# MLP block products on one NeuronCore: joined 512-column matmuls, sums on GpSimd, and a reordered tail

## The chip, the cores and the metric

The kernel runs on one core of a Trainium2 chip. Its time is the device time of one execution in microseconds (us). All inputs are laid out on the host beforehand and lie in the chip's memory; the output is written there.

## The reference

One layer of an encoder: a mixing block, then an MLP, then a final RMSNorm, for 512 tokens of width 2048, in float32. The change touches the MLP and the final norm only.

```python
h = h + mixed @ w_out
hn = _rmsnorm(h, norm_mlp_w)
h = h + jnp.square(jax.nn.relu(hn @ w_mlp_up)) @ w_mlp_down     # 2048 -> 8192 -> 2048
return _rmsnorm(h, norm_final_w)
```

## The kernel before

Everything is held transposed: features lie on the 128 partitions, the 512 tokens along the free axis. To keep float32 precision with fast matmuls, each operand is split into a rounded part (hi) and the remainder (lo), and a product is hi x hi + hi x lo + lo x hi. `split` does it: ScalarE casts the tile to hi, VectorE subtracts hi from the tile and writes lo (lines 94, 95).

**The MLP is computed by blocks.** Two blocks of weights' rows by two of columns (A11, A12, A21, A22) meet two halves of 256 tokens. Seven products of sums of blocks take the place of eight products of blocks: Q4, P1, P5, P6, P3, P7, P2. The weights' sums S1 to S4 are four VectorE additions of 128x1024 tiles (`run_product`), and each of the seven operands is split. The other side of a product is a tile `XS` of 128x512: columns 0 to 255 (`lo_t`) hold the hi part of one operand, columns 256 to 511 (`hi_t`) its lo part. `product` runs 8 contraction steps j, each with three matmuls of 256 columns: weights hi by X hi (line 904), the same weights hi by X lo (line 905), weights lo by X hi (line 906). All three add up in the same 256 columns of a PSUM bank. A pair has three banks, a, b and c, in which several products accumulate one after the other; after each product the bank's running value is read out.

**Up** (2048 to 8192): 32 pairs u0 to u31, one after the other (the first two and the last two interleaved). `up_evac` reads each product out: ScalarE copies Q4, P5, P1 and P6 into `tA` and `tB`, VectorE adds P7, P3 and P2 to those straight out of PSUM into the results `r0` and `r1`. VectorE then applies relu and the norm's factor `rB`, ScalarE squares. `differences` forms on VectorE the sums of token halves that the down projection needs, and the SyncE queue writes them to memory (`hidD`).

**Down** (8192 to 2048): 4 rounds b of 8 pairs, two pairs at a time. At a round's beginning `operand_fill` loads 56 tiles of 128x256 from `hidD` and splits them into `XS`. Each product is added by VectorE out of PSUM to a tile `h0` or `h1` (loaded from `hTD`) and stored back by `store`, in the last round also squared and summed into `acc`. The last two pairs of the last round (`keep`) run in another order, and `tail` and `finish` follow them with the final norm, half by half: the four tiles' squares, their column sums on TensorE (`stat2`), the reciprocal root on VectorE, then 16 scaled tiles of 128x256, five by GpSimd (line 1148) and eleven by VectorE (line 1150), and 16 DMAs to `out` on the SyncE queue (line 1151).

Tiles come from pools with a fixed number of buffers (3 for each of `wh` and `wl`, the split weights; 7 for `a`, the second row of weight blocks). Each engine takes its instructions in one fixed order, which is set when the program is built, from the data's dependences and from the free buffers; an instruction whose input or buffer is not ready holds up what stands behind it on its engine.

Of the kernel before, what the change touches and what calls it, by code (L numbers as in the profile page):

```python
# [49 lines left out]
def tile_hybrid_block(  # L50
# [733 lines left out]
    with ExitStack() as p1:  # L784
# [76 lines left out]
        with ExitStack() as p5:  # L861
# [36 lines left out]

            def product(ps, w, o, first=False):
                hi, lo = w  # L900
                for j in range(8):
                    t = XS[o, j]
                    c = slice(j * 128, (j + 1) * 128)
                    PE.matmul(ps, hi[:, c], t[:, lo_t], start=first and j == 0, stop=False, skip_group_check=True)  # L904
# [16 lines left out]
            def open_pair(nm, a11, a12):  # L921
                p = Pair()
                p.nm, p.ps, p.step = nm, {}, 0
                p.a11, p.a12 = a11, a12
                p.keep = False
                return p

            def run_product(p, q, sums):
# [27 lines left out]
                if bk not in p.ps:  # L956
                    p.ps[bk] = bank()[:, 0:256]
                product(p.ps[bk], w, ROLE[q], q in FIRST)
                return p.ps[bk]

# [7 lines left out]

            def up_evac(i, p, q, et):
                ps = p.ps[BANK[q]]  # L970
                if not hasattr(p, "tA"):
                    p.tA, p.tB = et(f"tA_u{i}"), et(f"tB_u{i}")
                    p.r0, p.r1 = ev(f"r0_u{i}"), ev(f"r1_u{i}")
                    p.left = 7
                tA, tB, r0, r1 = p.tA, p.tB, p.r0, p.r1
                if q == "Q4":
                    S_.copy(out=tA[:, 0], in_=ps)
                elif q == "P5":
                    S_.copy(out=tA[:, 1], in_=ps)
                elif q == "P1":  # L980
                    S_.copy(out=tB[:, 0], in_=ps)
                elif q == "P6":
                    S_.copy(out=tB[:, 1], in_=ps)  # L983
                elif q == "P7":
                    add(r1.rearrange("p (o t) -> p o t", o=2), ps[:, None, :].to_broadcast([128, 2, 256]), tA)
                    V.scalar_tensor_tensor(out=r1, in0=r1, scalar=0.0, in1=rB, op0=ALU.min, op1=ALU.mult)
                    S_.activation(out=r1, in_=r1, func=AF.Square)
                elif q == "P3":
                    add(r0[:, hi_t], ps, tB[:, 1])
# [31 lines left out]
            for i, p in enumerate(first):  # L1021
                for q in ("P1", "P2"):
                    w = heads[i, q] or wsplit(p.a12, f"{q}_u{i}")
                    p.ps[BANK[q]] = bank()[:, 0:256]
                    product(p.ps[BANK[q]], w, ROLE[q], True)
# [3 lines left out]
        with ExitStack() as p6:  # L1029
            sm = p6.enter_context(tc.tile_pool(name="sm", bufs=1, side="right", reuse_waits="tile"))  # L1030

            def a_tile(name):
                return sm.tile([128, 1024], F32, tag="a", name=name, bufs=7)

            def et(name):
                return sm.tile([128, 2, 256], F32, tag="et", name=name, bufs=6)

            def more(p, s22, s21):
# [4 lines left out]
            def up_group(idx, order, ps=None):  # L1043
                ps = ps or [up_open(i) for i in idx]
                for i, p in zip(idx, ps):
                    m0, m1 = up_m(i)
                    more(p, wup[m1, 1], wup[m1, 0])
                if order[0] == "P1":
                    for q in ("P1", "P2"):
                        for i, p in zip(idx, ps):  # L1050
                            up_evac(i, p, q, et)
                    order = order[2:]
                for n, q in enumerate(order):
                    for i, p in zip(idx, ps):
# [24 lines left out]
            def down_group(b, idx, order, done):  # L1079
                ps = []  # L1080
                for i in idx:
                    p = open_pair(f"d{b}_{i}", load_raw(wdn[2 * i, 2 * b], f"A11_d{b}_{i}"), load_raw(wdn[2 * i, 2 * b + 1], f"A12_d{b}_{i}"))
                    more(p, wdn[2 * i + 1, 2 * b + 1], wdn[2 * i + 1, 2 * b])
                    p.keep = order is not ORDER
                    ps.append(p)
                for e in (1, 0):
# [57 lines left out]
            def finish(half, ts, sqs):  # L1144
                psf = yield from stat2(f"f{half}", sqs, range(2 * half, 2 * half + 2))
                for m in range(16):
                    if m % 3 == 2:
                        G.tensor_tensor(out=Hf[m][:, ts], in0=Hf[m][:, ts], in1=rB[:, ts], op=ALU.mult)
                    else:
                        V.tensor_tensor(out=Hf[m][:, ts], in0=psf[:, ts], in1=Hf[m][:, ts], op=ALU.mult)  # L1150
                    nc.sync.dma_start(out=out[m * 128 : (m + 1) * 128, ts], in_=Hf[m][:, ts])
                    if half == 0 and m % 4 == 3:
                        yield
# [15 lines left out]
            def tail(i, p, q):  # L1169
                if i != 7 or q not in ("P2", "P3"):  # L1170
                    return
                half = 0 if q == "P2" else 1
                ts = slice(half * 256, half * 256 + 256)
                sqs = []
                for k, x in enumerate(pairs):
                    for e, h in ((0, x.h0), (1, x.h1)):
                        m = 2 * (6 + k) + e
                        sq = tp.tile([128, T], F32, tag="sq", name=f"sqt{m}{half}", bufs=1)
                        S_.activation(out=sq[:, ts], in_=h[:, ts], func=AF.Square)
                        if m < 15:  # L1180
                            add(acc[:, ts], acc[:, ts], sq[:, ts])
                        else:
                            sqs.append(sq)
# [4 lines left out]
                tasks.append(finish(half, ts, sqs))  # L1188

# [95 lines left out]
```

## Time and profile before

| | |
|---|---|
| median of 3 runs | 2886.01 us (2880.28 to 2888.11) |
| the profiled execution, whole | 2884.02 us |
| its span in the trace | 2881.9 us |
| TensorE busy | 2811.9 us, 98% |
| VectorE busy | 2065.1 us, 72% |
| ScalarE busy | 1167.0 us, 40% |
| GpSimd busy | 24.8 us, 1% |

The rows further down come from the profiled execution; its time is 2.0 us below the median of the runs. PE is TensorE's matmuls, PEld its weight loads, DVE VectorE, ACT ScalarE, POOL GpSimd, SPq the DMA issues of SyncE. An instruction's duration is longer than the distance to the next one behind it where the two overlap, so for a rate the distance between starts is read. "Idle ... <-" names what ended a wait.

### The profile page before, as it was taken

To read this page: it belongs to the slowest core of one execution; us is meant where nothing else is said; L and a number is where in the kernel's file an instruction comes from. 1 tells how busy PE (TensorE), PEld (TensorE's weight loads), DVE (VectorE), ACT (ScalarE), POOL (GpSimd) and SP (SyncE) were. 2 spreads that over 40 slices of the span, in tenths; PEclk is the share of its full clock that TensorE was granted. 3 is DMA by queue.
4 is the path that set the end of the run, shared out by engine and by line. 5 is a ranking of instruction groups with operands and counts; after the bars stand their busy time and mean duration, and the time that the engine had idled before them with its cause. 6 is when DMAs were issued, how large, how long until landed. Compare 5 with 4: busy or idle time off the path is not lost.

```text
span 2881.9 us, 45456 instructions
## 1 busy us (share of the span) xinstructions
PE 2811.9 (98%) x17944; PEld 2538.3 (88%) x17944; DVE 2065.1 (72%) x3131; ACT 1167.0 (40%) x1869; POOL 24.8 (1%) x66
## 2 busy tenths in 40 slices
PE   8999999999999999999999999999998999999997
PEld 6778788888788888888888999999998999999997
DVE  6888769845564444444447888888888888898987
ACT  6444322223233333322335444444445354444543
POOL 0000010000000000000000000000000000000000
PEclk9999999999999999999999999999999999999998
DMA  7555663555642222533443445454447566565644
GB/s 228 191 187 189 196 198 120 183 173 182 181 140 93 87 93 84 199 133 125 142 145 137 153 151 156 143 162 147 149 146 228 180 222 201 170 226 174 221 133 146
DMA packets 217493, 469.32 MB, mean 163 GB/s; under 512 B 38976, under 2 KB 80000, under 8 KB 217280
## 3 DMA queue, kind: packets, MB, share of 16 engines
q1 hardware_dynamic: 216608, 464.33, 49.9%
q8 instruction: 140, 2.29, 0.3%
q0 software_dynamic: 672, 2.10, 0.3%
q14 instruction: 73, 0.60, 0.1%
HBM read 379.15 MB, written 87.20 MB: 162 GB/s over the span
## 4 chain that ended last, share of the span: by engine, by line
PE 78%; DMA 9%; DVE 9%; ACT 2%; issue 1%; SPq 0%; DVEq 0%; ACTq 0%
PE ps_b L906 12%; PE ps_b L904 12%; PE ps_b L905 12%; PE ps_mm L115 8%; PE ps_mm L117 8%; PE ps_mm L116 8%; PE ps_b L115 4%; PE ps_b L116 4%; PE ps_b L117 4%; DMA hr<-hidD 1%; DVE wl_S_d L95 1%; DVE wl_in L90 1%; DMA bB<-rowD 1%; DMA hTD<-h 1%; DMA Nd<-bB 1%
## 5 line engine op out<-in xcount | busy, mean ns | idle before, releaser
L115 PE MATMUL ps_mm<-xh,wh_in 128*128 128x512 f32 x1416 | 567.1, 400 | 3.1 <-ACT wh_in L89 3.1
L117 PE MATMUL ps_mm<-xh,wl_in 128*128 128x512 f32 x1416 | 559.9, 395 | 0.5 <-DVE wl_in L90 0.5
L116 PE MATMUL ps_mm<-xl,wh_in 128*128 128x512 f32 x1416 | 559.8, 395 | 0.0
L89 ACT CAST wh_in<-raw_in 128x1024 fp32r<-128x1024 f32 x177 | 186.0, 1051 | 412.9 <-PE ps_mm L116 328.5
L117 PEld LDWEIGHTS ps_mm<-xh,wl_in 128*128 128x128 f32 x1416 | 267.7, 189 | 60.4 <-DVE wl_in L90 1.0
L115 PEld LDWEIGHTS ps_mm<-xh,wh_in 128*128 128x128 f32 x1416 | 267.7, 189 | 58.6 <-ACT wh_in L89 3.5
L116 PEld LDWEIGHTS ps_mm<-xl,wh_in 128*128 128x128 f32 x1416 | 267.7, 189 | 55.0 <-issue 0.2
L90 DVE TENSOR_TENSOR wl_in<-raw_in,wh_in 128x1024 fp32r<-128x1024 f32 x177 | 216.2, 1222 | 118.7 <-ACT wh_in L89 110.2
L904 PE MATMUL ps_b<-XT_h,wh_S_d 128*128 128x256 f32 x768 | 220.8, 287 | 10.6 <-ACT wh_S_d L94 10.6
L906 PE MATMUL ps_b<-XT_h,wl_S_d 128*128 128x256 f32 x768 | 220.9, 288 | 3.2 <-DVE wl_S_d L95 3.1
L905 PE MATMUL ps_b<-XT_h,wh_S_d 128*128 128x256 f32 x768 | 219.8, 286 | 0.0
L906 PE MATMUL ps_b<-XT_x,wl_S_u 128*128 128x256 f32 x768 | 217.4, 283 | 0.8 <-DVE wl_S_u L95 0.8
L904 PE MATMUL ps_b<-XT_x,wh_S_u 128*128 128x256 f32 x768 | 217.4, 283 | 0.5 <-ACT tB_u L983 0.5
L905 PE MATMUL ps_b<-XT_x,wh_S_u 128*128 128x256 f32 x768 | 217.3, 283 | 0.0
L94 ACT CAST wh_S_u<-A_u 128x1024 fp32r<-128x1024 f32 x128 | 134.3, 1050 | 147.2 <-DVE A_u L911 81.2
L94 ACT CAST wh_S_d<-A_d 128x1024 fp32r<-128x1024 f32 x124 | 129.6, 1047 | 148.2 <-PE ps_b L905 129.0
L95 DVE TENSOR_TENSOR wl_S_u<-A_u,wh_S_u 128x1024 fp32r<-128x1024 f32 x128 | 156.0, 1222 | 39.4 <-ACT wh_S_u L94 39.4
L95 DVE TENSOR_TENSOR wl_S_d<-A_d,wh_S_d 128x1024 fp32r<-128x1024 f32 x124 | 151.2, 1222 | 23.9 <-ACT wh_S_d L94 22.2
L904 PEld LDWEIGHTS ps_b<-XT_h,wh_S_d 128*128 128x128 f32 x768 | 149.8, 195 | 12.5 <-ACT wh_S_d L94 12.5
L906 PEld LDWEIGHTS ps_b<-XT_h,wl_S_d 128*128 128x128 f32 x768 | 149.9, 195 | 5.0 <-DVE wl_S_d L95 5.0
L905 PEld LDWEIGHTS ps_b<-XT_h,wh_S_d 128*128 128x128 f32 x768 | 149.9, 195 | 0.0
L906 PEld LDWEIGHTS ps_b<-XT_x,wl_S_u 128*128 128x128 f32 x768 | 147.2, 192 | 1.0 <-DVE wl_S_u L95 1.0
(393 smaller groups left out, 7033.9 us busy)
## 6 DMA issues: line engine op xcount, KB each, us to landing
raw_in<-in_win SPq DMA_DIRECT2D x177, 512.0 KB
raw_A_u<-in_wup SPq DMA_DIRECT2D x64, 512.0 KB
A_u<-in_wup SPq DMA_DIRECT2D x64, 512.0 KB
A_d<-in_wdn SPq DMA_DIRECT2D x64, 512.0 KB
raw_A_d<-in_wdn SPq DMA_DIRECT2D x64, 512.0 KB
raw_wo<-in_wout SPq DMA_DIRECT2D x32, 512.0 KB
h<-hTD SPq DMA_DIRECT2D x64, 256.0 KB
hTD<-h SPq DMA_DIRECT2D x60, 256.0 KB
```

The lines of the kernel that those rows point to most:

```text
L89: S_.copy(out=hi, in_=raw)
L90: V.tensor_tensor(out=lo, in0=raw, in1=hi.bitcast(F32), op=ALU.subtract)
L94: S_.copy(out=hi, in_=src)
L95: V.tensor_tensor(out=lo, in0=src, in1=hi.bitcast(F32), op=ALU.subtract)
L115: PE.matmul(ps, hi[:, w], rh, start=first and kk == 0, stop=False)
L116: PE.matmul(ps, hi[:, w], rl, start=False, stop=False)
L117: PE.matmul(ps, lo[:, w], rh, start=False, stop=last and kk == 7)
L904: PE.matmul(ps, hi[:, c], t[:, lo_t], start=first and j == 0, stop=False, skip_group_check=True)
L905: PE.matmul(ps, hi[:, c], t[:, hi_t], start=False, stop=False, skip_group_check=True)
L906: PE.matmul(ps, lo[:, c], t[:, lo_t], start=False, stop=j == 7, skip_group_check=True)
```

## The change

- **Joined matmuls.** In `product` (new argument `whole`), the two matmuls with the weights' hi part become one of 512 columns over the whole `XS` tile; its result fills a whole bank, hi x hi in the first half and hi x lo in the second. The third stays at 256 columns and adds into the first half. In the last contraction step the two change places.
- **Read-out.** Each of these products is now copied whole (128x512) by ScalarE into a new tile `u` (`spill`, two buffers), and GpSimd (`gsum`, a tensor_tensor) adds up the two halves: per up pair 9 adds of 128x256 and one of 128x512, per down pair 13 and one. VectorE's adds out of PSUM go. This holds for all 32 up pairs and the first 30 down pairs; the last two (`keep`) stay as they were.
- **Buffers.** `a` has 6 buffers where it had 7.
- **Tail.** `tail` takes the square of each of the last four tiles' halves when that half is complete; it no longer scales those four by `nfw_s` on ScalarE. In `finish`, VectorE does this scaling in a scalar_tensor_tensor for tiles 12 to 15, GpSimd has four tiles and VectorE twelve, and in the second half every other output DMA is issued by ScalarE's queue.

```diff
+                    if whole:
+                        mms = [(ps, hi, t), (ps[:, lo_t], lo, t[:, lo_t])]
+                        for n, (dst, a, b) in enumerate(mms if j < 7 else mms[::-1]):
+                            PE.matmul(dst, a[:, c], b, start=first and j + n == 0, stop=j == 7 and n == 1, skip_group_check=True)
...
+            def gsum(out, x, y, op=ALU.add):
+                G.tensor_tensor(out=out, in0=x, in1=y, op=op)
...
+                u = spill(ps, f"u{q}_u{i}")
                 if q == "Q4":
-                    S_.copy(out=tA[:, 0], in_=ps)
+                    gsum(tA[:, 0], u[:, 0], u[:, 1])
                 elif q == "P5":
-                    S_.copy(out=tA[:, 1], in_=ps)
+                    gsum(tA[:, 1], u[:, 0], u[:, 1])
                 elif q == "P7":
-                    add(r1.rearrange("p (o t) -> p o t", o=2), ps[:, None, :].to_broadcast([128, 2, 256]), tA)
+                    gsum(u[:, 0], u[:, 0], u[:, 1])
+                    gsum(r1.rearrange("p (o t) -> p o t", o=2), u[:, 0:1, :].to_broadcast([128, 2, 256]), tA)
...
-                    add(r0[:, lo_t], ps, tB[:, 0])
+                    dst = r0[:, lo_t] if q in ("P1", "P2") else r0[:, hi_t]
+                    gsum(dst, dst if q in ("P2", "P3") else u[:, 1], u[:, 0])
+                    if q in ("P2", "P3"):
+                        gsum(dst, dst, u[:, 1])
...
-                return sm.tile([128, 1024], F32, tag="a", name=name, bufs=7)
+                return sm.tile([128, 1024], F32, tag="a", name=name, bufs=6)
...
+            def spill(ps, name):
+                u = sm.tile([128, 2, 256], F32, tag="pr", name=name, bufs=2)
+                S_.copy(out=u.rearrange("p a b -> p (a b)"), in_=ps)
+                return u
...
+                        if p.whole:
+                            u = spill(t, f"u{q}_{p.nm}")
+                            if q == "P7":
+                                gsum(u[:, 0], u[:, 0], u[:, 1])
+                                hv = h1.rearrange("p (o t) -> p o t", o=2)
+                                gsum(hv, hv, u[:, 0:1, :].to_broadcast([128, 2, 256]), ALU.subtract)
+                            else:
+                                dst = (h1 if q in ("Q4", "P5") else h0)[:, lo_t if q in ("Q4", "P1", "P2") else hi_t]
+                                for k in range(2):
+                                    gsum(dst, dst, u[:, k], ALU.subtract if q in ("Q4", "P5") else ALU.add)
...
+                    queue = nc.scalar if half and m % 2 else nc.sync
+                    queue.dma_start(out=out[m * 128 : (m + 1) * 128, ts], in_=Hf[m][:, ts])
...
-                        S_.activation(out=h[:, ts], in_=h[:, ts], func=AF.Copy, scale=nfw_s[:, m : m + 1])
-                        Hf[m] = h
+                sq = tp.tile([128, T], F32, tag="sq", name=f"sqt{m}{half}", bufs=1)
+                S_.activation(out=sq[:, ts], in_=h[:, ts], func=AF.Square)
+                Hf[m] = h
```

On TensorE, inside an up product, two contraction steps stand like this before (`wh` and `wl` are the weights' hi and lo parts, `XT_x` the operand):

```order
L904 MATMUL ps_b<-XT_x_12070,wh_S_u_14219 128x256
L905 MATMUL ps_b<-XT_x_12070,wh_S_u_14219 128x256
L906 MATMUL ps_b<-XT_x_12070,wl_S_u_14220 128x256
L904 MATMUL ps_b<-XT_x_12071,wh_S_u_14219 128x256
L905 MATMUL ps_b<-XT_x_12071,wh_S_u_14219 128x256
L906 MATMUL ps_b<-XT_x_12071,wl_S_u_14220 128x256
```

And now, the last two steps of a product and the first of the next:

```order
L907 MATMUL ps_b<-XT_x_12052,wh_A_u_14722 128x512
L907 MATMUL ps_b<-XT_x_12052,wl_A_u_14723 128x256
L907 MATMUL ps_b<-XT_x_12053,wl_A_u_14723 128x256
L907 MATMUL ps_b<-XT_x_12053,wh_A_u_14722 128x512
L907 MATMUL ps_b<-X_x_10839,wh_A_u_14750 128x512
L907 MATMUL ps_b<-X_x_10839,wl_A_u_14751 128x256
```

Three matmuls of 256 columns a step have become one of 512 and one of 256.

On ScalarE, from the read-out of Q4 to that of P6 of one up pair, before (a name's ending `_u26` is the pair; casts make `wh`):

```order
L977 COPY tA_u26_18313<-ps_b_18288 128x256 [waits DMAHW3_49,PE_49]
L996 ACTIVATE r0_u25_18080<-r0_u25_18080 128x512 [waits DMAHW0_49,DVE_49]
L94 CAST wh_S2_u26_18389<-A22_u26_18280 128x1024 [waits DVE_49,Activation_49]
L981 COPY tB_u26_18314<-ps_b_18322 128x256 [waits DMAHW4_49,PE_49]
L94 CAST wh_S4_u26_18419<-A22_u26_18280 128x1024 [waits DVE_49,Activation_49]
L979 COPY tA_u26_18313<-ps_b_18353 128x256 [waits PE_49]
L94 CAST wh_S3_u26_18449<-A21_u26_18281 128x1024 [waits Activation_49]
L94 CAST wh_A12_u26_18480<-raw_A12_u26_18278 128x1024 [waits DMAHW0_49,PE_49,Activation_49]
L983 COPY tB_u26_18314<-ps_b_18322 128x256 [waits PE_49]
```

And now, from the read-out of Q4 to that of P3:

```order
L1050 COPY uQ4_u21_16315<-ps_b_16294 128x512 [waits PE_49,Activation_49]
L94 CAST wh_S2_u21_16377<-A22_u21_16286 128x1024 [waits DVE_49]
L1050 COPY uP1_u21_16339<-ps_b_16322 128x512 [waits PE_49,Activation_49]
L94 CAST wh_S4_u21_16401<-A22_u21_16286 128x1024 [waits DVE_49]
L1050 COPY uP5_u21_16364<-ps_b_16347 128x512 [waits PE_49,Pool_49]
L94 CAST wh_S3_u21_16426<-A21_u21_16287 128x1024
L1050 COPY uP6_u21_16397<-ps_b_16322 128x512 [waits PE_49,Pool_49]
L94 CAST wh_A12_u21_16452<-raw_A12_u21_16284 128x1024 [waits DMAHW2_49]
L1050 COPY uP3_u21_16421<-ps_b_16347 128x512 [waits PE_49,Pool_49]
```

A copy of 512 columns stands between any two casts, and from the third on it waits for GpSimd, which must have read the buffer of two products earlier; the casts stand behind it.

GpSimd had no instruction in the MLP before. Now it has, for one up pair (`tA` collects for `r1`; each `u` is a copied product):

```order
L978 TENSOR_TENSOR tA_u24_16899<-uQ4_u24_16903 128x256 [waits DMAHW0_49,Activation_49]
L978 TENSOR_TENSOR r0_u24_16901<-uP1_u24_16927 128x256 [waits DMAHW6_49,DVE_49,Activation_49]
L978 TENSOR_TENSOR tA_u24_16899<-uP5_u24_16952 128x256 [waits Activation_49]
L978 TENSOR_TENSOR r0_u24_16901<-uP6_u24_16985 128x256 [waits Activation_49]
L978 TENSOR_TENSOR r0_u24_16901<-r0_u24_16901,uP3_u24_17009 128x256 [waits Activation_49,Pool_49]
L978 TENSOR_TENSOR r0_u24_16901<-r0_u24_16901,uP3_u24_17009 128x256 [waits Pool_49]
L978 TENSOR_TENSOR uP7_u24_17034<-uP7_u24_17034 128x256 [waits Activation_49]
L978 TENSOR_TENSOR r1_u24_16902<-uP7_u24_17034,tA_u24_16899 128x512 [waits DMAHW7_49,DMAHW3_49,Pool_49]
L978 TENSOR_TENSOR r0_u24_16901<-r0_u24_16901,uP2_u24_17060 128x256 [waits Activation_49]
L978 TENSOR_TENSOR r0_u24_16901<-r0_u24_16901,uP2_u24_17060 128x256 [waits Pool_49]
```

Ten adds, all with both inputs and the output in SBUF.

## Rows read from the trace of the kernel before

**Rows 1.** The page, part 1: busy time, share of span, instructions of each engine.
```profile
PE 2811.9 (98%) x17944; PEld 2538.3 (88%) x17944; DVE 2065.1 (72%) x3131; ACT 1167.0 (40%) x1869; POOL 24.8 (1%) x66
```

**Rows 2.** The page, part 4: the chain that ended last, by engine.
```profile
PE 78%; DMA 9%; DVE 9%; ACT 2%; issue 1%; SPq 0%; DVEq 0%; ACTq 0%
```

**Rows 3.** Stretches of up and of down: length, busy by engine, clock, DMA share, GB/s.
```profile
1640.00:2200.00 560.00, 560.00 (x4676) 559.85 (x4674) 476.27 (x576) 273.25 (x379) 0.00 (x0) 1.00 0.49 156
2200.00:2845.00 645.00, 629.70 (x5160) 625.33 (x5160) 565.49 (x776) 305.25 (x443) 0.00 (x0) 0.99 0.59 191
```

**Rows 4.** Waits of TensorE, 1640 to 2845 us: total, times, longest.
```profile
PE ps_b L904 <- ACT wh_S_d L94: 11.7, 11, 2.4
```

**Rows 5.** Timeline of TensorE in the MLP, 24 matmuls apart: start, duration, instruction.
```profile
2609.89 0.28 PE L904 MATMUL ps_b<-X_h,wh_A_d 128*128 128x256 f32 x1
...
2612.77 0.28 PE L904 MATMUL ps_b<-X_h,wh_A_d 128*128 128x256 f32 x1
```

**Rows 6.** The same in two 512-column stretches, 15 and 24 matmuls apart.
```profile
1201.61 0.40 PE L115 MATMUL ps_b<-ybh,wh_pb 128*128 128x512 f32 x1
...
1205.11 0.39 PE L115 MATMUL ps_b<-ybh,wh_pb 128*128 128x512 f32 x1
...
1400.04 0.39 PE L115 MATMUL ps_b<-mh,wh_wo 128*128 128x512 f32 x1
...
1405.48 0.39 PE L115 MATMUL ps_b<-mh,wh_wo 128*128 128x512 f32 x1
```

**Rows 7.** VectorE's groups, 23 up pairs: xcount | busy, mean ns | idle before.
```profile
L95 DVE TENSOR_TENSOR wl_S_u<-A_u,wh_S_u 128x1024 fp32r<-128x1024 f32 x92 | 112.2, 1222 | 26.9 <-ACT wh_S_u L94 26.9
L911 DVE TENSOR_TENSOR A_u<-A_u,raw_A_u 128x1024 f32<-128x1024 f32 x69 | 84.2, 1221 | 0.8
L911 DVE TENSOR_TENSOR r_u<-ps_b,tB_u 128x256 f32<-128x256 f32 x45 | 19.0, 422 | 15.6 <-PE ps_b L906 15.6
```

**Rows 8.** Timeline of VectorE in an up pair.
```profile
1886.08 0.69 DVE L986 SCALAR_TENSOR_TENSOR r_u<-r_u,rB 128x512 f32<-128x512 f32 x1
1886.68 1.22 DVE L911 TENSOR_TENSOR A_u<-A_u,raw_A_u 128x1024 f32<-128x1024 f32 x1
1887.82 0.42 DVE L911 TENSOR_TENSOR r_u<-ps_b,tB_u 128x256 f32<-128x256 f32 x1
1888.15 1.22 DVE L95 TENSOR_TENSOR wl_S_u<-A_u,wh_S_u 128x1024 fp32r<-128x1024 f32 x1
```

**Rows 9.** Timeline of GpSimd and VectorE in the final norm's second half.
```profile
2870.81 2.78 POOL L1148 TENSOR_TENSOR Hf<-Hf,rB 128x256 f32<-128x256 f32 x4 [9.53 <-ACT rB L1166]
...
2870.76 2.74 DVE L1150 TENSOR_TENSOR Hf<-ps_b,Hf 128x256 f32<-128x256 f32 x8 [1.72 <-ACT rB L1166]
```

**Rows 10.** Timeline of GpSimd at the start.
```profile
0.74 0.20 POOL masks.py:197 MEMSET ident<- 128x128 f32 x1 [0.29 <-POOLq L1274]
...
1.77 0.53 POOL L323 MEMSET rst<- 128x512 f32 x1
```

**Rows 11.** ScalarE's groups, around and in the up pairs.
```profile
L840 ACT COPY rB<-ps_b 128x512 f32<-128x512 f32 x1 | 0.6, 585 | 1.1 <-PE ps_b L149 1.1
L94 ACT CAST wh_S_u<-A_u 128x1024 fp32r<-128x1024 f32 x92 | 96.6, 1050 | 106.7 <-DVE A_u L911 63.6 <-PE ps_b L905 43.1
L977 ACT COPY tA_u<-ps_b 128x256 f32<-128x256 f32 x23 | 8.6, 374 | 31.7 <-PE ps_b L906 31.7
```

**Rows 12.** The tail: chain pieces, SyncE's output issues, one stretch as in Rows 3.
```profile
2861.76 0.33 DVE h L911
...
2862.46 0.42 ACT sqt L1179
...
2864.39 1.85 PE ps_s L1161 x8
...
2871.56 5.76 SPq L1151 DMA_DIRECT2D out<-Hf  x12
...
2876.00:2878.00 2.00, 0.00 (x0) 0.00 (x0) 0.00 (x0) 0.00 (x0) 0.00 (x0) 0.50 0.80 268
```

More of the change, by code (lines that the diff above doesn't have):

```diff
@@ L897, in wsplit, with product @@
                 return split(raw, hi, lo)
-            def product(ps, w, o, first=False):
+            def product(ps, w, o, first=False, whole=True):
                 hi, lo = w
@@ L903, in product @@
                     c = slice(j * 128, (j + 1) * 128)
+                    if whole:
+                        mms = [(ps, hi, t), (ps[:, lo_t], lo, t[:, lo_t])]
+                        for n, (dst, a, b) in enumerate(mms if j < 7 else mms[::-1]):
+                            PE.matmul(dst, a[:, c], b, start=first and j + n == 0, stop=j == 7 and n == 1, skip_group_check=True)
+                        if j % NPUMP == NPUMP - 1:
+                            pump()
+                        continue
                     PE.matmul(ps, hi[:, c], t[:, lo_t], start=first and j == 0, stop=False, skip_group_check=True)
@@ L925, in open_pair @@
                 p.keep = False
+                p.whole = True
                 return p
@@ L956, in run_product @@
                 if bk not in p.ps:
-                    p.ps[bk] = bank()[:, 0:256]
-                product(p.ps[bk], w, ROLE[q], q in FIRST)
+                    p.ps[bk] = bank() if p.whole else bank()[:, lo_t]
+                product(p.ps[bk], w, ROLE[q], q in FIRST, p.whole)
                 return p.ps[bk]
@@ L967, in up_open, with up_evac @@
                 return open_pair(f"u{i}", load_raw(wup[m0, 0], f"A11_u{i}"), load_raw(wup[m0, 1], f"A12_u{i}"))
-            def up_evac(i, p, q, et):
+            def gsum(out, x, y, op=ALU.add):
+                G.tensor_tensor(out=out, in0=x, in1=y, op=op)
+            def up_evac(i, p, q, et, spill):
                 ps = p.ps[BANK[q]]
@@ L1023, in tile_hybrid_block @@
                     w = heads[i, q] or wsplit(p.a12, f"{q}_u{i}")
-                    p.ps[BANK[q]] = bank()[:, 0:256]
+                    p.ps[BANK[q]] = bank()
                     product(p.ps[BANK[q]], w, ROLE[q], True)
@@ L1050, in up_group @@
                         for i, p in zip(idx, ps):
-                            up_evac(i, p, q, et)
+                            up_evac(i, p, q, et, spill)
                     order = order[2:]
@@ L1055, in up_group @@
                         run_product(p, q, a_tile)
-                        up_evac(i, p, q, et)
+                        up_evac(i, p, q, et, spill)
                     if n == 2:
@@ L1084, in down_group @@
                     p.keep = order is not ORDER
+                    p.whole = not p.keep
                     ps.append(p)
@@ L1146, in finish @@
                 for m in range(16):
-                    if m % 3 == 2:
+                    if m % 3 == 2 and m < 12:
                         G.tensor_tensor(out=Hf[m][:, ts], in0=Hf[m][:, ts], in1=rB[:, ts], op=ALU.mult)
-                    else:
-                        V.tensor_tensor(out=Hf[m][:, ts], in0=psf[:, ts], in1=Hf[m][:, ts], op=ALU.mult)
-                    nc.sync.dma_start(out=out[m * 128 : (m + 1) * 128, ts], in_=Hf[m][:, ts])
+                    elif m < 12:
+                        V.tensor_tensor(out=Hf[m][:, ts], in0=psf[:, ts], in1=Hf[m][:, ts], op=ALU.mult)
+                    else:
+                        V.scalar_tensor_tensor(out=Hf[m][:, ts], in0=psf[:, ts], scalar=nfw_s[:, m : m + 1], in1=Hf[m][:, ts], op0=ALU.mult, op1=ALU.mult)
+                    queue = nc.scalar if half and m % 2 else nc.sync
+                    queue.dma_start(out=out[m * 128 : (m + 1) * 128, ts], in_=Hf[m][:, ts])
                     if half == 0 and m % 4 == 3:
@@ L1169, in tail @@
             def tail(i, p, q):
-                if i != 7 or q not in ("P2", "P3"):
+                ends = {"P7": (0, 1), "P2": (0, 0), "P5": (1, 1), "P3": (1, 0)}
+                if q not in ends:
                     return
-                half = 0 if q == "P2" else 1
+                half, e = ends[q]
+                h, m = (p.h0, p.h1)[e], 2 * i + e
                 ts = slice(half * 256, half * 256 + 256)
[L1174 to L1183, printed above, removed]
-                        S_.activation(out=h[:, ts], in_=h[:, ts], func=AF.Copy, scale=nfw_s[:, m : m + 1])
-                        Hf[m] = h
+                sq = tp.tile([128, T], F32, tag="sq", name=f"sqt{m}{half}", bufs=1)
+                S_.activation(out=sq[:, ts], in_=h[:, ts], func=AF.Square)
+                Hf[m] = h
+                if m != 14:
+                    add(acc[:, ts], acc[:, ts], sq[:, ts])
+                    return
                 if half == 0:
                     reload()
-                tasks.append(finish(half, ts, sqs))
+                tasks.append(finish(half, ts, [sq]))
             pairs = []
```

8 lines of the change are left out of this document (1 added, 7 removed).

## The prediction

> **What bounds the kernel now.** I read the busy shares first, then the chain, then the MLP's stretches, its waits, and last the distances between starts. TensorE is busy 98% of the span and GpSimd 1% [rows 1]; TensorE also carries 78% of the chain that ended last [rows 2]. In the up stretch it is busy all 560 us, in the down stretch 629.7 of 645 [rows 3], and the largest sum of its waits there, 11.7 us, is for ScalarE's casts [rows 4]. So the MLP runs at TensorE's rate, at full clock (1.00 and 0.99 of 2.4 GHz). But VectorE is close behind: 476 of 560 us and 565 of 645 [rows 3], 85% and 88%. Whatever makes VectorE 15% slower per pair becomes the bound. That is the second thing to watch.
>
> The rate: 24 matmuls of 256 columns, one product, take 2.88 us, 0.120 each [rows 5]. A pair of seven products takes 20.16 us, a down pair with its share of the waits (15.3 us over some 32 pairs) 20.6. A 512-column matmul comes every 0.2267 us in one stretch and every 0.2333 in another [rows 6]. Twice 0.120 is 0.240: each matmul carries about 13 ns besides its columns, and joining two saves one such piece.
>
> I sum against the profiled execution's 2884 us (2 under the median of the runs, inside their spread). A difference of 0.3%, 8.7 us, is about what a measurement of this kernel can tell from none.
>
> **The change, part by part.**
>
> *TensorE.* 32 up and 30 down pairs with 7 products each are 434 products. A new one takes 8 x (0.2267 + 0.120) = 2.773 us, 0.107 less: -46 us if TensorE still sets the pace. With 0.2333 it is -23. I take the first, measured in the stretch just ahead of the MLP. A pair then asks for 19.4 us.
>
> *ScalarE.* Seven copies of 128x512 at 0.585 us (the one such copy out of PSUM) instead of four of 0.374, beside seven casts at 1.05 [rows 11]: 11.5 us of a pair's 19.4, with two squares below 13. Nothing on the path by itself. But each copy now waits for GpSimd to have read the buffer of two products ago, and the next cast stands behind it. So a late GpSimd reaches TensorE through ScalarE's queue.
>
> *VectorE* loses two adds of 128x256 and one of 128x512 in an up pair, six and one in a down pair: by the distances 0.33 and 0.60 [rows 8] 1.3 and 2.6 us. Alone this buys only the down phase's waits, at most 15 us. What stays: 11 operations of 128x1024 a pair (seven splits, four sums; in 23 up pairs 92 of S splits and 69 of sums [rows 7], 4 and 3 a pair) at a distance of 1.14, two of 128x512 at 0.60 and four of 128x256 at 0.34 [rows 8]: 15.1 us an up pair. A down pair has the eleven and a share of the operand splits, 56 in 8 pairs, seven at 0.34: 14.9. Nearly all have both inputs in SBUF.
>
> *GpSimd.* Its add of 128x256 comes every 0.695 us (2.78 for four) [rows 9]; one of 128x512 doesn't occur, so at most twice that, 1.39. An up pair: 9 x 0.695 + 1.39 = 7.7 us; a down pair: 13 x 0.695 + 1.39 = 10.4. Against 19.4 it has room, if it works at this pace.
>
> *Side by side or by turns.* This decides the sign. The trace has GpSimd's adds only beside VectorE operations that take one input out of PSUM (`psf`): there both run at their own pace [rows 9]. It has no GpSimd add beside a VectorE operation with both inputs in SBUF, and those are all that VectorE does in the changed MLP. One hint: GpSimd needs 0.695 us for a tile for which VectorE needs 0.34, so it seems to fetch two inputs one after the other through one path. From both sides: fully side by side, TensorE's 19.4 us hold. Fully by turns, a pair needs the sum:
> - by distances, up 15.1 + 7.7 = 22.8 (+2.6 to 20.16, x 32 = +84), down 14.9 + 10.4 = 25.3 (+4.7 to 20.6, x 30 = +141), and in six pairs of the last round two more adds into `acc` at 0.60, +7: +232 us.
> - by the columns' part alone. VectorE's is (1.14 - 0.34) / 768 = 1.04 ns a column, so 0.07 us an operation is fixed; GpSimd's fixed part, by its memsets, is 0.20 - (0.53 - 0.20) / 3 = 0.09 [rows 10]. If fixed parts overlap the other engine's work, 17 x 0.07 + 10 x 0.09 = 2.1 us go from an up pair, 18 x 0.07 + 14 x 0.09 = 2.5 from a down pair: 20.7 and 22.8, so +17, +66, +7: +90 us.
>
> By turns lies in between. I start at the lower end, since on one engine the fixed parts do overlap (an operation lasts 1.22 us, the next starts after 1.14 [rows 8]), and add that each of the 32 x 10 + 30 x 14 = 740 GpSimd adds breaks VectorE's overlap once, 0.08 us: +59. That is +149 us. I take turns over side by side because nothing in the trace bears out a full overlap, and a gain needs much of it: it pays only if over a third of GpSimd's time in up (2.6 of 7.7) and almost half in down (4.7 of 10.4) runs free beside VectorE.
>
> The Trainium skill speaks against this change here: SBUF — State Buffer, "Who interferes with whom", says that a VectorE instruction with two SBUF inputs and a GpSimd instruction that reads SBUF contend for a shared read port, whichever begins first holding it for its whole length. By that rule the sums by turns above are the result; no row of this trace shows such a pair of instructions, and the row with the PSUM input agrees with what the section says of one SBUF input.
>
> *Buffers and the step from up to down.* `a` with six tiles still holds three pairs' second rows of weights; DMA is half busy [rows 3], nothing. The last up pair's read-out grows from one add to a copy and two adds, some 1.6 us on the way to the down operands: +2.
>
> *Tail.* At present the last product's read-out at 2861.76 to 2862.1 is followed by squares and adds until the column sums start at 2864.39; with one square (0.42) left [rows 12] they start some 1.8 us sooner. The 16 output DMAs are issued about 0.48 us apart (5.76 for 12) while the DMA engines are 0.80 busy [rows 12]: two queues could bring 0 to 2 us, one more VectorE tile costs 0.34. Together -3 us (0 to -4).
>
> **The rivals.**
>
> *Forecast, by turns:* 2884 + 149 + 2 - 3 = 3032 us; between its ends (+90, +232) 2973 and 3115. TensorE would then be idle some 10 to 15% of the MLP.
>
> *Free side by side, faster:* VectorE and GpSimd each at their pace. Then 2884 - 46 + 2 - 3 = 2837 us (2860 with the 0.2333 distance, 2827 if the down waits go as well). It speaks for it that the two shared the final norm without loss [rows 9], and that GpSimd has half its time left. It decides if GpSimd's adds stay below some 1.2 us and VectorE's 128x1024 below 1.2 apart.
>
> *Only GpSimd stretched:* VectorE goes first and GpSimd works in what is left, at about half pace: up 15.4 us (fits, -0.75 x 32 = -24), down 20.8 (+0.2 x 30 = +6). 2884 - 18 - 1 = 2865 us.
>
> *The joined matmul saves nothing*, because the two matmuls of a step, now of unequal length, come 0.36 us apart together as three did: 2884 - 1 = 2883 us, if nothing else interferes. The 512-column stretches speak against it: there weights change with each matmul as well [rows 6].
>
> The Trainium skill's page TensorE: Matmul & The Clock Gate, "Back-to-back issue gap", gives N / 2.4 + 2.5 ns a matmul; by it, joining would save 2.5 ns a step, an estimate of 9 us in all, not 46. The rows here show 13 ns over the columns, and they decide.
>
> **How the numbers follow.** By turns 0.56, free 0.30, GpSimd alone stretched 0.08, joined for nothing 0.06. By turns ends slower except where the ports are freer than my lower end (0.02 of it to no difference). Free is faster. A stretched GpSimd is faster in 0.06 and slower in 0.02; joined for nothing is within 0.3% in 0.04, slower in 0.02. Faster by over 0.3%: 0.36; within: 0.06; slower: 0.58. Time: that of the likeliest, 3032 us, its own range 2973 to 3115. The range for 8 in 10 has to take in the free case from 2832 on and by turns up to 3100, which leaves out the ends of both, about 2 in 10.
>
> **What would show it.** Distances between starts: joined step 0.347 us, right or wrong for the TensorE term. GpSimd's 128x256 adds in the MLP: 0.70 us long means free, 1 us and more means turns; VectorE's 128x1024 splits: 1.22 means free, longer ones or gaps of half a microsecond that end with a GpSimd add mean turns. Idle TensorE waiting for `wl` (VectorE) or `wh` (ScalarE) in the MLP would be 100 us and more by turns, below 20 if free. ScalarE's copies waiting for GpSimd would show the way of the delay. The forecast is wrong if VectorE keeps its 1.14 us distance while GpSimd works.

## The result

The changed kernel takes 3090.43 us (median of 4, 3085.83 to 3096.05), the kernel before beside it 2883.66: a ratio of 1.0724, interval 1.0703 to 1.0745, so 7.2% slower. The forecast by turns was 3032 us, with 2973 to 3115 as its own range.

The page of the changed kernel, part 1 (busy time by engine) and the first line of part 4 (the chain), beside [rows 1, 2]:

```profile
PE 2858.4 (92%) x14472; PEld 2357.7 (76%) x14472; DVE 2235.1 (72%) x2827; ACT 1334.6 (43%) x2167; POOL 986.3 (32%) x804
...
PE 42%; DVE 20%; issue 19%; POOL 8%; DMA 6%; ACT 4%; SPq 0%; DVEq 0%; POOLq 0%; ACTq 0%
```

VectorE has 304 instructions fewer and is busy 170 us more. TensorE's share of the chain fell from 78% to 42%; VectorE, GpSimd and issue have what it lost.

Stretches of up and of down in the changed kernel (columns as in [rows 3]):

```profile
1640.00:2250.00 610.00, 548.38 (x2916) 455.46 (x2916) 508.40 (x443) 306.74 (x417) 314.33 (x261) 0.97 0.41 129
...
2600.00:3040.00 440.00, 385.39 (x2083) 313.09 (x2082) 388.29 (x325) 245.20 (x390) 348.12 (x257) 0.99 0.49 159
```

TensorE now stands still for 61.6 of 610 us in up and 54.6 of 440 in down, where [rows 3] had 0 of 560 and 15.3 of 645. The granted clock of the up stretch, 0.97 where it was 1.00, isn't what makes it long: it is 0.93 from 1725 to 1800 us and 1.00 from 1800 to 1900, and the pairs of both take 23.4 to 23.5 us. Where the 212.4 us between the two spans lie, from the starts of the same instructions in both traces:

| stretch | before | after | difference |
|---|---|---|---|
| start to the first up pair's relu | 575.2 | 583.0 | +7.8 |
| first to last up pair's relu | 609.9 | 707.7 | +97.8 |
| from there to the first down store | 51.4 | 71.5 | +20.1 |
| first to last down store | 585.4 | 678.1 | +92.7 |
| from there to the end | 60.1 | 54.0 | -6.1 |

An up pair takes 23.45 us where it took 20.13. A part of one, on VectorE and then on GpSimd (start, duration, instruction, idle time before it):

```profile
1902.99 1.21 DVE L95 TENSOR_TENSOR wl_S_u<-A_u,wh_S_u 128x1024 fp32r<-128x1024 f32 x1
1904.13 0.41 DVE L918 TENSOR_TENSOR tA_u<-r_u 128x256 f32<-128x256 f32 x1
1904.46 1.76 DVE L918 TENSOR_TENSOR A_u<-A_u,raw_A_u 128x1024 f32<-128x1024 f32 x1
...
1907.34 1.23 DVE L95 TENSOR_TENSOR wl_S_u<-A_u,wh_S_u 128x1024 fp32r<-128x1024 f32 x1
1908.60 1.65 DVE L918 TENSOR_TENSOR A_u<-A_u,raw_A_u 128x1024 f32<-128x1024 f32 x1
```

```profile
1904.29 0.85 POOL L978 TENSOR_TENSOR tA_u<-uQ_u 128x256 f32<-128x256 f32 x1 [2.90 <-ACT uQ_u L1050]
1907.87 1.29 POOL L978 TENSOR_TENSOR r_u<-uP_u 128x256 f32<-128x256 f32 x1 [2.73 <-ACT uP_u L1050]
```

The two 128x1024 operations that begin while a GpSimd add is running (1904.46 and 1908.60) last 1.76 and 1.65 us, the others 1.21 and 1.23. The add that begins while a split is running (1907.87) lasts 1.29 where four together took 2.78 in [rows 9], and that split keeps its 1.23: whichever comes second is drawn out. The groups over the up stretch say the same (xcount | busy, mean ns | idle before):

```profile
L95 DVE TENSOR_TENSOR wl_S_u<-A_u,wh_S_u 128x1024 fp32r<-128x1024 f32 x104 | 133.4, 1283 | 37.2 <-ACT wh_S_u L94 34.3
L918 DVE TENSOR_TENSOR A_u<-A_u,raw_A_u 128x1024 f32<-128x1024 f32 x79 | 132.6, 1678 | 1.8
L95 DVE TENSOR_TENSOR wl_A_u<-raw_A_u,wh_A_u 128x1024 fp32r<-128x1024 f32 x52 | 89.8, 1728 | 0.0
```

GpSimd's most frequent add, in down:

```profile
L978 POOL TENSOR_TENSOR h<-h,uP_d 128x256 f32<-128x256 f32 x300 | 413.2, 1387 | 112.7 <-ACT uP_d L1050 100.8
```

The weights' sums, 1.22 us in [rows 7], take 1.68, GpSimd's adds 1.39 where they took 0.70. How the delay travels stands in the waits (total, times, longest; MLP):

```profile
ACT wh_S_u L94 <- DVE A_u L918: 120.9, 56, 2.5
...
ACT uP_d L1050 <- POOL h L978: 100.6, 66, 2.9
```

```profile
PE ps_b L907 <- DVE wl_A_u L95: 53.5, 30, 1.8
PE ps_b L907 <- DVE wl_S_d L95: 40.1, 48, 2.4
PE ps_b L907 <- DVE wl_A_d L95: 32.3, 43, 3.2
PE ps_b L907 <- DVE XT_h L95: 19.6, 1, 19.6
```

A late sum delays its cast, the cast its split, and TensorE waits for `wl`; in down ScalarE's copies wait for GpSimd as well. The last row, a single wait of 19.6 us, is another matter (below).

### The profile page after: what moved, and what is told of

Read it like the earlier page. It is cut to its first block, busy times and chain, and to the rows that moved or that the text cites. A ratio compares the mean times of both kernels' runs of the same rounds, so it can differ in the third digit from the quotient of the medians.

```text
span 3094.3 us, 39922 instructions
## 1 busy us (share of the span) xinstructions
PE 2858.4 (92%) x14472; PEld 2357.7 (76%) x14472; DVE 2235.1 (72%) x2827; ACT 1334.6 (43%) x2167; POOL 986.3 (32%) x804
## 4 chain that ended last, share of the span: by engine, by line
PE 42%; DVE 20%; issue 19%; POOL 8%; DMA 6%; ACT 4%; SPq 0%; DVEq 0%; POOLq 0%; ACTq 0%
PE ps_b L907 12%; PE ps_mm L115 8%; PE ps_mm L116 8%; PE ps_mm L117 8%; DVE wl_S_d L95 3%; POOL r_u L978 3%; POOL h L978 3%; DVE A_d L918 2%; DVE wl_S_u L95 2%; DVE A_u L918 2%; DVE wl_A_d L95 2%; POOL uP_u L978 2%; DVE wl_A_u L95 1%; DVE XT_h L95 1%; DVE X_h L95 1%
## 5 line engine op out<-in xcount | busy, mean ns | idle before, releaser
L978 POOL TENSOR_TENSOR h<-h,uP_d 128x256 f32<-128x256 f32 (+1 forms) x330 | 464.8, 1419 | 115.0 <-ACT uP_d L1050 100.8
L907 PE MATMUL ps_b<-XT_x,wh_S_u 128*128 128x512 f32 x768 | 275.0, 398 | 1.8 <-ACT wh_S_u L94 1.8
L907 PE MATMUL ps_b<-XT_h,wh_S_d 128*128 128x512 f32 x720 | 263.7, 409 | 6.0 <-ACT wh_S_d L94 6.0
L978 POOL TENSOR_TENSOR r_u<-uP_u 128x256 f32<-128x256 f32 x64 | 88.0, 1376 | 526.7 <-ACT uP_u L1050 522.8
L907 PE MATMUL ps_b<-XT_h,wl_S_d 128*128 128x256 f32 x720 | 196.6, 294 | 29.6 <-DVE wl_S_d L95 29.3
L95 DVE TENSOR_TENSOR wl_S_d<-A_d,wh_S_d 128x1024 fp32r<-128x1024 f32 x124 | 189.6, 1538 | 28.8 <-ACT wh_S_d L94 28.8
L907 PE MATMUL ps_b<-X_x,wh_A_u 128*128 128x512 f32 x480 | 187.4, 419 | 0.0
L1050 ACT COPY uP_d<-ps_b 128x512 f32<-128x512 f32 x180 | 105.3, 585 | 181.6 <-POOL h L978 100.6
L907 PE MATMUL ps_b<-X_x,wl_A_u 128*128 128x256 f32 x480 | 134.7, 302 | 50.7 <-DVE wl_A_u L95 50.7
L907 PE MATMUL ps_b<-X_h,wh_A_d 128*128 128x512 f32 x480 | 172.0, 398 | 2.3 <-ACT wh_A_d L94 2.3
```

The source lines that it names most:

```text
L95: V.tensor_tensor(out=lo, in0=src, in1=hi.bitcast(F32), op=ALU.subtract)
L907: PE.matmul(dst, a[:, c], b, start=first and j + n == 0, stop=j == 7 and n == 1, skip_group_check=True)
L978: G.tensor_tensor(out=out, in0=x, in1=y, op=op)
L1050: S_.copy(out=u.rearrange("p a b -> p (a b)"), in_=ps)
```

## The experiments

Each ran beside the kernel before on the same chip.

**Adds that nothing waits for.** Does GpSimd alone do it, or the chain of copies and adds? The kernel before, with two GpSimd adds per product:

```diff
+                for k in range(2):
+                    c = slice(256 * k, 256 * k + 256)
+                    G.tensor_tensor(out=x[:, c], in0=h[:, c], in1=h[:, c], op=ALU.add)
```

> The kernel before (with six buffers of a, as in the change), and beside each product two GpSimd adds of 128x256 into a tile that nobody reads. Nothing waits for their result; a weight buffer waits for them only three products later. By turns: 14 x 0.70 = 9.8 us a pair on top of VectorE's 15 to 17.5 us with two SBUF inputs make 25 to 27 us a pair for TensorE's 20.2: 3080 to 3250 us. If both engines work at their own pace: 2884 us within 9.

3018.52 us, ratio 1.0467 (1.0441 to 1.0494): 137 us for work that is no one's input. VectorE's groups in up (1640 to 2150):

```profile
L95 DVE TENSOR_TENSOR wl_S_u<-A_u,wh_S_u 128x1024 fp32r<-128x1024 f32 x91 | 130.1, 1431 | 27.3 <-ACT wh_S_u L94 27.3
L911 DVE TENSOR_TENSOR A_u<-A_u,raw_A_u 128x1024 f32<-128x1024 f32 x67 | 106.7, 1593 | 0.8
```

So GpSimd's adds slow VectorE by running beside it. An up pair takes 22.60 us. Of VectorE's old 16.4 us, 15.1 have two SBUF inputs; by turns these and 14 adds of 0.695 are 24.8, and 22.4 without the fixed parts (17 x 0.07 and 14 x 0.09). What was found lies near this lower end, and the 3080 us and more that I expected came from adding full lengths.

**Writes only, and one input.** Two memsets of 128x512 per product, into the `lo` tile that the split then writes over, or, at the place of the idle adds, two copies of 128x256 (the last line):

```diff
+                    for k in range(2):
+                        G.memset(lo[:, 512 * k : 512 * k + 512].bitcast(F32), 0.0)
...
+                    G.tensor_copy(out=x[:, c], in_=h[:, c])
```

> As e3_idle_adds, but GpSimd fills the lo tile with zeros (two memsets of 128x512, about 0.53 us each) before VectorE writes the real values over them: GpSimd is busy some 7.4 us a pair and writes SBUF, but reads nothing. If it is reading that goes by turns: 2884 us within 12. If any work of GpSimd holds up VectorE's operations with two SBUF inputs: 23 to 25 us a pair, 3000 to 3150 us.

> The kernel before with two idle GpSimd copies of 128x256 per product, from the weights' hi part into a tile that nobody reads: one input in SBUF instead of the two of the idle adds, which gave 3018 us, and of the none of the idle fills, which gave 2884.6. If any read of SBUF by GpSimd makes VectorE wait for the instruction's whole length, the cost goes with GpSimd's busy time: a copy should last less than an add's 0.70 us, at 0.35-0.5 us some 50-75% of the adds' 137 us, 2950-2990 us. If only GpSimd instructions with two SBUF inputs take turns with VectorE: 2880-2890 us.

The fills: 2884.59 us, ratio 1.0011 (0.9996 to 1.0025), nothing. The copies: 2910.99 us, 1.0100 (1.0086 to 1.0115), a fifth of what the adds cost. GpSimd's fills in up, then copies and splits in the copies' kernel:

```profile
L899 POOL MEMSET wl_S_u<- 128x512 f32 x200 | 99.0, 524 | 188.1 <-PE ps_b L911 188.1
```

```profile
L967 POOL COPY xP_u<-wh_S_u 128x256 f32<-128x256 f32 x201 | 180.6, 931 | 192.9 <-ACT wh_S_u L94 190.2 <-ACT tA_u L989 2.6
...
L95 DVE TENSOR_TENSOR wl_S_u<-A_u,wh_S_u 128x1024 fp32r<-128x1024 f32 x100 | 135.1, 1352 | 29.8 <-ACT wh_S_u L94 29.8
```

The fills keep their 0.53 us ([rows 10]) for hundreds of times, and an up pair still takes 20.13 us. A copy that reads one input is drawn out and makes the split 0.13 us longer; reading is what collides. My range for the copies was too high: they last 0.93 us on average where two with nothing in their way took 0.74 together, so it is mostly they that wait. The fills' kernel also has six `a` buffers, so these cost nothing.

**VectorE with one input in PSUM.** The reverse: GpSimd's adds, ScalarE's copies and the joined matmuls of the changed kernel stay, and VectorE's 128x1024 operations take one of two inputs from PSUM. The kernel leaves out the subtraction of the hi part and the sums' first operand, so a split no longer waits for its cast.

```diff
+                    S_.copy(out=hi, in_=raw)
+                    halves(lo, raw, ALU.subtract)
...
+                V.tensor_tensor(out=o, in0=i, in1=CST[0][:, None, :].to_broadcast([128, 2, 512]), op=op)
```

> The changed kernel, but in the MLP's whole pairs from u2 on every VectorE split and every weight sum takes one of its two inputs from a constant tile in PSUM instead of SBUF; so the subtraction of the hi part and the sums' first operand are left out. GpSimd's adds, ScalarE's copies and the joined matmuls stay as in the changed kernel. If VectorE and GpSimd take turns because VectorE has both inputs in SBUF: GpSimd's 128x256 adds fall from 1.39 us to 0.70-0.80, VectorE's 128x1024 operations show one length near 1.22, and the time falls from 3090 to 2850-2910. If any VectorE work beside GpSimd does it: adds stay at 1.3-1.4 us and the time at 3070 or more. If the longer read-out (copy, then adds, two spill buffers) costs what the adds on VectorE still lost: 2930-2980, with adds at 0.70-0.80.

2883.76 us, ratio 1.0013 (1.0000 to 1.0027): the loss is gone. The engines' row and VectorE's groups in up, GpSimd's adds in down:

```profile
1640.00:2150.00 510.00, 510.00 (x2899) 443.91 (x2898) 399.03 (x438) 313.15 (x416) 212.83 (x260) 1.00 0.45 154
```

```profile
L907 DVE TENSOR_TENSOR wl_S_u<-A_u,ps_c 128x1024 fp32r<-128x1024 f32 x102 | 124.2, 1218 | 5.7 <-DVE A_u L907 0.5
L907 DVE TENSOR_TENSOR A_u<-raw_A_u,ps_c 128x1024 f32<-128x1024 f32 x75 | 91.1, 1215 | 0.0
...
L994 POOL TENSOR_TENSOR h<-h,uP_d 128x256 f32<-128x256 f32 x290 | 219.6, 757 | 191.1 <-ACT uP_d L1066 176.8 <-DMA hr<-hidD 2.9
```

One length of 1.22 us on VectorE, 0.76 on GpSimd, TensorE never idle in up. With one VectorE instruction more, the rest equal in number, and the same read-out chain, 7.1 of the 7.2% have gone with VectorE's second SBUF input and with the splits' wait for the casts (in the changed kernel 65 of 610 us in up). That wait was there before the change too and cost TensorE nothing in up, but what each of the two is worth on its own in the changed kernel this run doesn't tell.

The Trainium skill has this as a rule: SBUF — State Buffer, "Who interferes with whom", says that a VectorE instruction with two SBUF inputs contends with a GpSimd instruction that reads SBUF, not with one that only writes it, and that one SBUF input is free. All four runs agree: 137 us for the adds, 27 for the copies, none for the fills, none with the PSUM input.

**The same adds on VectorE.**

```diff
-                G.tensor_tensor(out=out, in0=x, in1=y, op=op)
+                V.tensor_tensor(out=out, in0=x, in1=y, op=op)
```

> The changed kernel with one word changed: the adds of the read-out run on VectorE, the busiest engine beside TensorE, instead of GpSimd; copies, buffers and their waits stay. By turns (VectorE with two SBUF inputs and GpSimd hold one path in turn): the adds cost VectorE 9 x 0.34 + 0.60 us an up pair and 13 x 0.34 + 0.60 a down pair, 18.8 and 19.9 us in all against 19.4 of TensorE, so some 2850 to 2875 us, over 200 us faster than on GpSimd. If the longer read-out itself (copy of 512 columns, two buffers, casts queued behind the copies) is what costs the time, it stays near 3090 us or above.

2974.24 us, ratio 1.0316 (1.0301 to 1.0331). VectorE does all of GpSimd's work and the kernel is 116 us faster for it. But it is 93 us slower than before, and an up pair takes 21.59 us. I expected 2850 to 2875, since VectorE's load, 15.1 + 9 x 0.34 + 0.60 = 18.8 us, is below TensorE's 19.7. The copies and adds of the read-out aren't it by themselves, since the PSUM kernel above has them too, if on GpSimd and without the splits' wait for the casts. The next three runs ask, for up, whether VectorE's load is.

**How much more VectorE can carry.** The kernel before with the new tail and joined matmuls in up alone, no spill, the extra half added by VectorE straight out of PSUM; for all seven products, or for `JOIN`:

```diff
+            JOIN = ("Q4", "P2")
...
+                    S_.copy(out=x, in_=ph if q in JOIN else pl)
+                    if q in JOIN:
+                        add(x, pl, x)
```

> The kernel before with joined matmuls in the up pairs alone, read out without the spill tile and without GpSimd: ScalarE copies 128x256 halves, VectorE adds the other halves straight out of PSUM (about 2.7 us a pair more on VectorE, 18.8-19.1 of the 19.7 that TensorE asks for). Down as before, the new tail. Adds on VectorE behind a spill copy took 20.9 us an up pair. If that loss came from the longer read-out (copy of 512, then adds, two buffers): an up pair now takes 19.6-19.9, the time is 2865-2875. If it came from VectorE being nearly full: 20.3-20.9 a pair again, the time 2885-2910.

> The kernel before with the new tail, and joined matmuls in the up pairs for Q4 and P2 alone, whose extra halves VectorE adds straight out of PSUM (2 more adds of 128x256 a pair, 0.68 us). Joining all seven that way took 2918 us. TensorE asks for 2 x 0.065 us a pair less, some 4 us in all, if joining saves per product what the join alone showed in up (13.6 us over 31 pairs of seven). If VectorE's slack (16.4 us of 20.2 busy) covers the adds: 2874-2880 us. If each VectorE operation between a product's cast and the next split delays TensorE, whatever the slack: 2890-2900 us (2/7 of the 38 us that joining seven lost).

> As with Q4 and P2, but also P5 and P3: 4 more adds of 128x256 a pair (1.36 us) on VectorE, its load some 17.8 of 19.9 us. If VectorE has room up to about 95%: -8 us by the joined matmuls, 2870-2877 us. If the delay goes with the number of added operations: 2895-2910 us.

| joined in up | VectorE's work a pair | an up pair takes | time | ratio, interval |
|---|---|---|---|---|
| none (before) | 16.4 | 20.13 | | |
| Q4, P2 | 17.1 | 20.05 | 2875.87 | 0.9977 (0.9968 to 0.9986) |
| Q4, P2, P5, P3 | 17.8 | 20.10 | 2877.80 | 0.9983 (0.9972 to 0.9995) |
| all seven | 18.8 | 21.35 | 2917.88 | 1.0124 (1.0100 to 1.0148) |

Joined for two, the kernel is 0.23% faster than the one before. Of the 10 us between their traces 4.4 lie behind the last down store, in the new tail; the 0.08 us a pair are lost again at the ends of the up stretch, which is as long as before from the first to the last pair's relu (610.0 against 609.9), so no gain from the joined matmuls is shown. Up to 17.8 us VectorE's work is hidden, at 18.8 it isn't, though TensorE would give it 19.7, and the time lies above both of my ranges. (The 20.9 us of the first expectation is the stretch from the first to the last relu over 31, which has other distances at its ends; counted so, joining all seven takes 20.8, in the second range.) VectorE's waits in the kernel that joins seven (1640 to 2150, 24 pairs) show a part of why:

```profile
DVE wl_S_u L95 <- ACT wh_S_u L94: 28.1, 24, 1.2
DVE tB_u L918 <- PE ps_b L907: 7.5, 24, 0.3
DVE tA_u L918 <- ACT tA_u L987: 6.2, 24, 0.3
```

Once a pair it waits 1.2 us for a cast, which itself waited for VectorE's sum: handing over between sum, cast and split leaves time that no other operation fills in the fixed order. With the smaller waits that is 2 us a pair. How this would go with another order wasn't tried.

**The join alone**, in the kernel before, with the old read-out from the first half of the bank (the second half, hi x lo, is left out):

```diff
-                return p.ps[bk]
+                return p.ps[bk][:, 0:256]
```

> The kernel before with the joined matmuls alone: a bank's first half is read out as before by ScalarE and VectorE, GpSimd has nothing to do. The hi x lo term, which lies in the second half, is left out of the MLP. If the TensorE term is right (0.347 us a contraction step, 434 products x 0.107 us), the time is 2884 - 46 = 2838 us. If the joined matmul saves nothing, 2883. If the 512-column distance is 0.233 in this stretch, 2860.

2871.15 us, ratio 0.9954 (0.9937 to 0.9970): -10, not -46. TensorE in up:

```profile
1900.21 0.40 PE L907 MATMUL ps_b<-XT_x,wh_A_u 128*128 128x512 f32 x1
1900.44 0.28 PE L907 MATMUL ps_b<-XT_x,wl_A_u 128*128 128x256 f32 x1
1900.56 0.40 PE L907 MATMUL ps_b<-XT_x,wh_A_u 128*128 128x512 f32 x1
1900.80 0.28 PE L907 MATMUL ps_b<-XT_x,wl_A_u 128*128 128x256 f32 x1
1900.92 0.40 PE L907 MATMUL ps_b<-XT_x,wh_A_u 128*128 128x512 f32 x1
```

Two steps take 0.71 us, one 0.355; over 1640 to 2150 us, 2906 matmuls in 510 us are 0.351 a step. Before, 4260 in the same stretch are 0.359. Seven products save 0.46 us, and the up pair fell from 20.13 to 19.67. Down gained nothing: 586.7 us from first to last store, where it was 585.4. TensorE's waits for `wh_S_d` grew from 11.7 ([rows 4]) to 17.2 us, and between those stores it stood still for 13.2 us instead of 6.4, at a granted clock of 0.99 instead of 1.00.

**The step from up to down.** In the changed kernel, the last two up pairs as before:

```diff
+                p.whole = i < 30
```

> The changed kernel with the last two up pairs as in the kernel before (three matmuls of 256 a step, no spill, VectorE adds out of PSUM). The step from up to down took 20 us more in the changed kernel where +2 was predicted. If the last pairs' read-out through ScalarE and GpSimd delays the down operands: the step falls from 71 us to 53-57 and the time from 3090 to 3070-3078. If the step is long because the operands' splits and the first down products themselves go by turns or wait for GpSimd's adds: 68-71 us still, time 3083-3090.

3073.08 us, ratio 1.0668 (1.0647 to 1.0688), and the step falls from 71.5 to 57.5 us. The trace puts the cause in SyncE's queue: the first load of a down operand from `hidD`, before, after and with the last pairs as before.

```profile
2159.22 0.32 SPq L1075 DMA_DIRECT2D hr0T<-hidD  x1
```

```profile
2305.73 0.45 SPq L1090 DMA_DIRECT2D hr0T<-hidD  x1
```

```profile
2262.18 5.31 SPq L1110 DMA_DIRECT2D hr0T<-hidD  x3
```

Before, it is issued 25.8 us ahead of the last up pair's relu (2185.04), and with the last pairs as before 23.3 us ahead of it (2285.45). In the changed kernel it is issued 15.1 us behind it (2290.67), since the queue's fixed order has it behind the last pairs' stores:

```
L1019 DMA hidD<-tA_u_18111 128x2x256 [waits DMAHW2_49,DVE_49]
L1020 DMA hidD<-tB_u_18112 128x256 [waits DMAHW3_49,DVE_49]
L1021 DMA hidD<-r_u_18113 128x256 [waits DMAHW4_49]
L1105 DMA h_3_18521<-hTD 128x512 [waits DMAHW5_49]
L1105 DMA h_0_18523<-hTD 128x512 [waits DMAHW7_49,DMAHW6_49]
L1090 DMA hr0T_18527<-hidD 128x512 [waits PE_49]
```

Hence the 19.6 us in which TensorE waits for `XT_h` (2.2 us with the last pairs as before). The same row stands behind the relu where GpSimd does no add (the VectorE kernel, step 67.5 us) and where it disturbs nobody (the PSUM kernel, 65.7), so this part has nothing to do with turns. Why the new read-out led to this order isn't shown, nor where the 6 us lie by which the step with the last pairs as before still exceeds the kernel before. TensorE's granted clock falls in the step in each of the three: 0.83 from 2205 to 2225 us before, 0.63 from 2290 to 2310 after, 0.61 from 2305 to 2325 with the last pairs as before.

**The tail alone**, on the kernel before:

```diff
+                ends = {"P7": (0, 1), "P2": (0, 0), "P5": (1, 1), "P3": (1, 0)}
...
+                    queue = nc.scalar if half and m % 2 else nc.sync
```

> The kernel before with the change in the tail alone (one square and one column-sum input left after the last read-out, scaling in the VectorE operation, output issues on two queues). Predicted -3 us (0 to -4): 2880, ratio 0.9990. Rival: the output is limited by the DMA engines and the squares were hidden, 2883-2884, ratio 1.000.

2879.14 us, ratio 0.9996 (0.9985 to 1.0007): the interval holds both answers. The trace is clearer. In the kernel with the tail alone, the last read-out, the column sums and the output issues:

```profile
2862.53 0.42 DVE L911 TENSOR_TENSOR h<-ps_b,h 128x256 f32<-128x256 f32 x1
...
2863.51 0.38 PE L1164 MATMUL ps_s<-ones,sqt 128*128 128x1 f32 x2 [0.95 <-ACT sqt L1180]
...
2869.68 3.37 SPq L1154 DMA_DIRECT2D out<-Hf  x6
...
2870.37 3.22 ACTq L1154 DMA_DIRECT2D out<-Hf  x6
```

From that read-out to the end of the span (2878.5) are 16.0 us; before, 20.2 (2861.68 to 2881.9), and in the changed kernel 16.0 (3078.27 to 3094.3).

## Why the prediction was right, and where it was off

*By turns*, right and shown: the idle adds bring 137 us of loss into the kernel before, and the fills, which read nothing, bring none. The PSUM input takes the loss out of the changed one (with the wait for the casts, as said). The signs I named came as told: adds of 1.39 us instead of 0.70, two lengths on VectorE, TensorE waiting for `wl` (138 us over the MLP, 100 and more forecast), ScalarE's copies waiting for GpSimd.

*Size, down*: near. 25.3 us a pair by distances, 22.8 by columns; 22.8 + 14 x 0.08 for broken overlaps = 23.9 was my value, in all +107 us with `acc`. Found: 20.6 x 678.1 / 585.4 = 23.9 a pair, +92.7 from first to last store.

*Size, up*: this term failed. I took 20.7 + 10 x 0.08 = 21.5 us a pair, +43 in all; found 23.45, above even the sum by distances, 22.8, and +97.8. These 55 us are most of what the forecast missed (18 more in the step to down, 8 at the start, less 14 in down and 3 at the end: 64 in all between forecast and trace). I sized only the sharing. VectorE's 17 operations are busy 19.5 us a pair here and 15.4 in the PSUM kernel (399.03 of 510 us at 19.72 a pair), so the sharing draws them out by 4.1 us. But VectorE also stands idle some 3.9 us in the pair at 1900 (busy 19.5 of 23.45), and that the sum left out (before, it stood idle 3.1 us a pair, but there TensorE set the pace). It waits for a cast, or for GpSimd, as in

```profile
DVE r_u L995 <- POOL r_u L978: 2.4, 2, 1.2
...
DVE wl_A_u L95 <- ACT wh_A_u L94: 1.2, 1, 1.2
```

(its waits from 1900 to 1923.45). It looks as if, on a chain that goes to and fro between engines, drawn-out operations add such waits. The kernels without GpSimd's adds that take 21.4 to 21.6 us with 18.8 us of VectorE work bear this out; how the 3.9 us divide between the two causes in the changed kernel isn't settled.

*The step from up to down*: +2 forecast, +20 found. I priced the last read-out and didn't read SyncE's queue at this place, where the order showed the operand loads moved behind the stores. The run that puts the last pairs back gives 14 of the 20 back.

*TensorE*: 0.347 us a step forecast, 0.351 found, and 0.359 before where I had 0.360. So a step saves 8 ns, not 13, and down gains nothing: -10 us, not -46. I had the slower distance in [rows 6] and took the faster one. The Trainium skill's formula (TensorE: Matmul & The Clock Gate, "Back-to-back issue gap") gave an estimate of 9 us; the total of the join alone is near that by luck: a step saves over three times its 2.5 ns, and up alone got 14 us shorter. The term isn't in the forecast by turns, but it carries the rival: *free side by side* was priced at 2837 us, and the PSUM kernel, in which it holds, takes 2884. Its up stretch is 12.1 us shorter (597.8), its step from up to down 14.3 longer. I gave 0.30 to a gain of 47 us; as far as the PSUM kernel shows, this change would have made no difference without turns.

*Start*: 7.8 us to the first up pair's relu were not forecast. The kernels with the spill copies in which GpSimd disturbs nobody have 5.6 of it (adds on VectorE, PSUM input), the join alone 0.2. I followed it no further.

*Tail*: -3 forecast, -4.2 in the traces; the timed runs can't tell it from none.

*Buffers*: six for `a` cost nothing, as said.

## What to carry to other kernels

GpSimd is no spare engine beside a VectorE whose operations read two SBUF tiles: here its adds cost more than the same adds on a VectorE that was already 85% busy. Let GpSimd only write, or let VectorE read one input from PSUM, and the two run side by side. Before moving work onto an engine, read what hands over to what (an engine at 18.8 of 19.7 us was already late), and read the DMA queue's order at every change of phase.

## What the runs showed of the hardware

- It looks like waiting, not like slower work: VectorE's 128x1024 operations last 1.21 to 1.23 us alone, and 1.47 to 1.81 where an add of GpSimd is in the way. One add of GpSimd lasted 4.11 us (at 2341.83) and one 9.22 us (at 2506.55) while VectorE ran on without a gap, so an engine can be passed over for several operations of the other.
- A GpSimd copy with one SBUF input still collides, but costs a fifth of what an add does (27 against 137 us for as many instructions).
- Steps that alternate 512 and 256 columns take 0.351 us, though [rows 5, 6] add up to 0.347 and 0.353.
